# First products by x block of 128 tokens, w2 in two loads, and an input verdict summed over a DMA row, in a Strassen ReGLU MLP kernel

## The chip, the cores and the metric

The kernel runs on one core of a Trainium2 chip. The metric is the device time of one execution in microseconds (us). The kernel before took 309.98 us, the median of its first three runs (309.86 to 310.02). Positions are microseconds from the start of the profiled span, which is about 1.8 us shorter than the time of the same execution.

## The reference

Shortened:

```python
def setup_inputs():
    batch, seq, dim, hidden = 16, 256, 512, 2048
    return {"x": randn(batch, seq, dim), "w1": randn(dim, hidden * 2), "w2": randn(hidden, dim)}   # all float32

def reference(x, w1, w2):
    h = x @ w1
    gate, value = np.split(h, 2, axis=-1)
    h = np.maximum(gate, 0) * value
    return (h @ w2).astype(np.float32)
```

So there are 4096 tokens, two matrix products, and a gate between them.

## The kernel before

The kernel computes both products in fp16 with Strassen-Winograd: seven half-size products P1 to P7 in place of eight, which needs sums of weights (T1 to T4) and sums of activations (S1 to S4). It goes through four stages of 1024 tokens. The first stage must also turn x on TensorE (transposes) and turn fp32 weights into fp16 operands while TensorE is already multiplying. Its first two blocks of hidden columns are therefore "Plain" blocks (ordinary products, no sums needed), and block 2 is the first Strassen block. The engines are scheduled by hand: the order of the calls is the order of each engine.

One Strassen block. ScalarE copies the first product X to Y, because both go on from it; TensorE's later products wait for that copy:

```python
        def P1(self):
            self.X = psx.tile([P, TH], F32, name="X", tag="X")
            self.mm("P1", self.X, True)
            self.Y = psy.tile([P, TH], F32, name="Y", tag="Y")
            nc.scalar.copy(out=self.Y, in_=self.X)
        # ... P5, P2, P6, P3, P7, P4: two products each, then one operation of ScalarE or VectorE
```

The start: the dummy products (TensorE work whose result nobody needs, done while it waits for its first loads), the loads, and the first Plain products of 256 or 512 columns:

```python
    for i in range(NWARM):                     # NWARM = 7
        nc.tensor.matmul(Y, warm_b[:, :P], warm_b[:, :TH], start=True, stop=True)
    # ...
    fetch_first(0, (0, 1))                     # x blocks of 128 tokens
    ws[0] = load_w1(nc.sync, *wl[0], (0,))     # gate weights of block 0
    fetch_first(0, (2, 3))
    load_w1(nc.sync, *wl[0], (1,))             # value weights of block 0
    fetch(1, nc.sync)
    # ...
    keep_busy(3)
    plain[0].open(W=False)
    plain[0].part("gate", *first_half, half)   # 256 columns: waits for two turned x blocks
    turn_first(xo, 0, 2, halves(*XS), (dve, act))
    turn_first(xo, 0, 3, halves(new_w(), new_w()), (dve, act))
    keep_busy(2)
    plain[0].part("gate", *first_half, other)
    # ... later: halves of the x sums, in this order of all four
    SUMS_X = {"S1": ("A21", "A22", ADD), "S2": ("S1", "A11", SUB), "S4": ("A12", "S2", SUB), "S3": ("A11", "A21", SUB)}
```

The streaming weights: GpSimd makes T1 to T4 of each chunk of w1, ScalarE casts the other three operands (`copy_some`), and w2 comes as four converting loads issued by GpSimd; two of GpSimd's subtractions make w2's T1 and T2:

```python
    if 5 <= todo < 9:
        n2 = ("B11", "T3", "B22", "B21")[todo - 5]
        nc.gpsimd.dma_start(out=vop[n2], in_=w2_v[(0, 0, 1, 1)[todo - 5], (0, 1, 1, 0)[todo - 5]])
    if (s, n, jb) == (0, "P7", 13):
        nc.gpsimd.tensor_tensor(vop["T1"], vop["T3"], vop["B11"], op=SUB)
        nc.gpsimd.tensor_tensor(vop["T2"], vop["B22"], vop["T1"], op=SUB)
```

The input verdict. The fp16 way is only right for inputs of ordinary size. Sums of squares are gathered in `st`; in the last stage they are judged, counted over the 128 partitions, and the program branches to a slow general way if any is out of range. With these inputs it never is. The count over partitions is a product of one column on TensorE:

```python
    def count(fit):
        n = P * st.shape[1]
        ps = psx.tile([P, TH], F32, name="X", tag="X")
        nc.tensor.matmul(ps[:1, :1], fit[:, :1], fit[:, 1:], start=True, stop=True)
        nc.vector.tensor_scalar(out=flag, in0=ps[:1, :1], scalar1=n - 0.5, scalar2=None, op0=LT)
    # ... in the last stage, at numbered steps of its second product:
            job(18, lambda: verdict.append(judge()))
            job(46, lambda: count(verdict[0]))
            job(78, lambda: verdict.append(nc.values_load(flag[0:1, 0:1], ...)))
```

Of the kernel before, what the change touches and what calls it, by code (L numbers as in the profile page):

```python
# [16 lines left out]
P = 128  # L17
# [79 lines left out]
def fast_way(ctx, tc, x2, w1, w2, out2, flag):  # L97
# [30 lines left out]
    w2_v = w2.rearrange("(u hc p) (v n) -> u v p hc n", u=2, v=2, p=P)  # L128
# [3 lines left out]
    vop = {n: wpool.tile([P, NJ // 2, DO // 2], F16, name=f"v_{n}") for n in ("B11", "B21", "B22", "T1", "T2", "T3", "T4")}  # L132
# [48 lines left out]
    def look_whole(t, at, of, half=False):  # L181

        sq = tmp.tile([P, 1024], F16, name="sq", tag="sq", bufs=1)
        nc.scalar.activation(sq[:, :of], t, SQUARE, scale=(P / of / (2 if half else 1)) ** 0.5,
                             accum_out=st[:, at:at + 1])
# [52 lines left out]
    class Block:  # L238
        def __init__(self, xo, g, jb):
            self.xo, self.g, self.jb = xo, g, jb  # L240
# [27 lines left out]
        def P3(self):  # L268
# [3 lines left out]
            nc.vector.scalar_tensor_tensor(out=self.c12, in0=self.W, scalar=GS, in1=self.u2, op0=MULT, op1=ADD)  # L272
            nc.vector.scalar_tensor_tensor(out=self.g[:, self.jb, :TH], in0=self.X, scalar=0.0,  # L273
                                           in1=self.c12, op0=MAX, op1=MULT)

        def P7(self):
            self.mm("P7", self.Y, False)
            nc.vector.scalar_tensor_tensor(out=self.c22, in0=self.Y, scalar=GS, in1=self.p5, op0=MULT, op1=ADD)  # L278
            second_halves()
# [170 lines left out]
    def plain_w(i):  # L450
        jb, n, _ = wl[i]
        t = ws.pop(i)
        js = slice(jb * P, (jb + n) * P)
        for n, k, v in (("B11", 0, 0), ("B21", 1, 0), ("T3", 0, 1)):
            nc.gpsimd.tensor_copy(out=wop[n][:, :, js], in_=t[:, k, :, v])
        return lambda: nc.scalar.copy(out=wop["B22"][:, :, js], in_=t[:, 1, :, 1])
# [49 lines left out]
    ws[0] = load_w1(nc.sync, *wl[0], (0,))  # L506
    fetch_first(0, (2, 3))
    load_w1(nc.sync, *wl[0], (1,))
    fetch(1, nc.sync)
# [10 lines left out]
    def halves(*ts):  # L520
        return [t[:, :2 * P] for t in ts]
# [4 lines left out]
    rest = plain_w(0)  # L526
    turn_first(xo, 0, 0, halves(*YS), (dve, act))
    XS = [new_x(), new_x()]
    turn_first(xo, 0, 1, halves(*XS), (dve, act))
    arm(YS[0])  # L530
    arm(YS[1])
    keep_busy(3)
    plain[0].open(W=False)
    plain[0].part("gate", *first_half, half)
    turn_first(xo, 0, 2, halves(*XS), (dve, act))
    turn_first(xo, 0, 3, halves(new_w(), new_w()), (dve, act))
    keep_busy(2)
    plain[0].part("gate", *first_half, other)
    plain[0].W = new_w()
    rest()  # L540
    rest = plain_w(1)
    plain[0].part("value", *first_half)
# [3 lines left out]
    rest()  # L546
    fetch(4, nc.sync)
    plain[0].gate(0)
    plain[1].part("value", *first_half)
    spare = plain[0].X, plain[1].W  # L550
    cast_first(0, pool)
    cast_first(1, dve)
    cast_first(2, pool)
    turn_first(xo, 1, 0, (turns(YS[0])[0], turns(YS[1])[0]), (dve, act))
    turn_first(xo, 1, 1, (turns(plain[0].X)[0], turns(plain[0].W)[0]), (dve, act))
    plain[1].value()
    held = plain[1].held(0)
    cast_first(3, dve)
    xo["S3"] = halfs.tile([P, 8, P], F16, name="xh", tag="xh").rearrange("p (a b) c -> p a (b c)", a=2)
    sums = [sums_of({n: t[:, :, slice(*c)] for n, t in xo.items()}) for c in (half, other)]  # L560
    next(sums[0])
    plain[0].open()
    plain[0].part("gate", *second_half, half)
    turn_first(xo, 1, 2, turns(spare[0]), (act, act))
    turn_first(xo, 1, 3, turns(spare[1]), (dve, dve))
    plain[0].part("value", *second_half, half)
    plain[1].open(*reversed(YS))
    plain[1].part("gate", *second_half, half)
    plain[1].part("value", *second_half, half)
    next(sums[1])  # L570
    next(sums[0])
    next(sums[1])
# [191 lines left out]
```

## Time and profile before

| | before |
|---|---|
| time, first three runs | 309.98 us |
| span of the profiled run | 308.2 us |
| TensorE busy | 301.5 us (98%), 1863 matmuls |
| last matmul ends | 303.50 us |
| end, counted from there ("the tail") | 4.65 us |

TensorE is the bound: the chain that ended last is 97% TensorE. The change removes no real product, so it can only win the holes between products. Those waits are few. TensorE's waits in the kernel before (what waited, for whom, total us, times, longest):

```profile
PE Y L145 <- DVE warm L141: 1.3, 1, 1.3
PE X L314 <- DVE x_S L488: 0.3, 1, 0.3
PE X L245 <- ACT Y L252: 0.3, 1, 0.3
```

The first is the program's own start. The third is the largest hole in the steady part. In the timeline of TensorE it looks like this (start, duration, engine, line, operation, idle before and its releaser); the starts go up by 0.43 us for two products of 512 columns, and then once by 0.85:

```profile
28.70 0.59 PE L245 MATMUL W<-x_S,w_T 128*128 128x512 f16 x2
29.13 0.60 PE L245 MATMUL Y<-xh,w_T 128*128 128x512 f16 x2
29.98 0.59 PE L245 MATMUL X<-x_A,w_B 128*128 128x512 f16 x2 [0.26 <-ACT Y L252]
```

Another hole, at 64.37, comes from a first sum of g (the gated hidden layer, the input of the second product) on VectorE that takes 1.38 us, while its fellows take 0.69. VectorE's timeline, kernel before:

```profile
62.93 1.38 DVE L165 TENSOR_TENSOR w_stage<-g 128x1024 f16<-128x1024 f16 x1
64.41 0.69 DVE L165 TENSOR_TENSOR w_stage<-w_stage,g 128x1024 f16<-128x1024 f16 x1
```

It runs beside this subtraction on GpSimd (GpSimd's timeline, same kernel), which ends at 63.76:

```profile
59.70 4.06 POOL L671 TENSOR_TENSOR v_T<-v_B,v_T 128x2048 f16<-128x2048 f16 x1
```

The Trainium skill, page "SBUF — State Buffer", section "Who interferes with whom", says that a VectorE instruction with two inputs in SBUF contends with a GpSimd instruction that reads SBUF, and that the one that issues second is blocked. This trace agrees that the second one is slowed: 1.38 us against 0.69.

### The profile page before, as it was taken

Reading aid. Unit: us, or ns where it says so; the run is one execution under the profiler, and the core shown is the slowest. Engines: PE = TensorE matmul, PEld = TensorE weight load, DVE = VectorE, ACT = ScalarE, POOL = GpSimd, SP = SyncE. Lnnn points to the kernel's source line nnn. Section 1 sums busy time; section 2 is a strip of 40 time slices with the busy share of each in tenths; the row PEclk is TensorE's granted clock in tenths of the full one; section 3 lists DMA queues with packets and bytes.
Section 4 is the critical chain, followed back from the end, with each engine's and each line's share of the span. In section 5 each row is a group of like instructions: output and inputs, shape, how many; then the busy total and the mean of one; then the engine's idle time right before and its main releaser. Section 6 shows DMA issues by size and latency. Waiting matters only on the chain.

```text
span 308.2 us, 5215 instructions
## 1 busy us (share of the span) xinstructions
PE 301.5 (98%) x1863; PEld 182.4 (59%) x1863; DVE 235.8 (77%) x383; ACT 176.7 (57%) x350; POOL 154.7 (50%) x192
## 2 busy tenths in 40 slices
PE   8999999999999999999999999999999999999993
PEld 5644444588844444478864444458884444448883
DVE  1589888889778888887537888889536888888841
ACT  2598885455865555537855555546865555553230
POOL 1399999920058999400028958910007988700000
PEclk9999999999999999999999999999999999999999
DMA  7977797983784143001354910000335110001132
GB/s 233 353 233 215 211 238 90 191 164 82 213 253 95 66 73 64 2 0 54 137 181 93 188 67 4 0 0 22 117 106 168 35 36 1 0 3 34 53 120 72
DMA packets 37916, 32.87 MB, mean 107 GB/s; under 512 B 14464, under 2 KB 33408, under 8 KB 37760
## 3 DMA queue, kind: packets, MB, share of 16 engines
q1 hardware_dynamic: 33536, 26.22, 28.0%
q0 software_dynamic: 4352, 6.29, 12.1%
q8 instruction: 15, 0.25, 0.4%
q14 instruction: 13, 0.11, 0.1%
HBM read 27.26 MB, written 12.58 MB: 129 GB/s over the span
## 4 chain that ended last, share of the span: by engine, by line
PE 97%; DVE 1%; ACT 0%; issue 0%; DVEq 0%
PE Y L245 26%; PE X L245 17%; PE W L245 17%; PE Y L351 14%; PE W L351 9%; PE X L351 8%; PE Y L145 1%; PE X L314 1%; PE W L314 1%; PE Y L314 1%; DVE w_stage L165 0%; PE X L485 0%; PE Y L485 0%; DVE x_A L488 0%; DVE g L288 0%; PE Y L502 0%
## 5 line engine op out<-in xcount | busy, mean ns | idle before, releaser
L245 PEld LDWEIGHTS <-w_T 128*128 128x128 f16 x496 | 48.4, 98 | 56.9 <-POOL w_T L227 0.3
L175 POOL TENSOR_TENSOR fold<-xh 128x1024 f32<-128x1024 f16 x16 | 30.3, 1894 | 92.2 <-DMA xh<-x 91.4
L245 PE MATMUL X<-x_A,w_B 128*128 128x512 f16 x248 | 73.8, 379 | 0.3 <-ACT Y L252 0.3
L245 PE MATMUL Y<-x_S,w_T 128*128 128x512 f16 x220 | 65.5, 379 | 0.0
L245 PEld LDWEIGHTS <-w_B 128*128 128x128 f16 x372 | 36.3, 98 | 42.6 <-issue 1.1
L272 DVE SCALAR_TENSOR_TENSOR cc<-W,pu 128x512 f32<-128x512 f32 x62 | 42.8, 691 | 20.4 <-ACT pu L266 19.6
L252 ACT COPY Y<-X 128x512 f32<-128x512 f32 x62 | 35.4, 570 | 38.0 <-PE X L245 37.7
L266 ACT ACTIVATE pu<-Y 128x512 f32<-128x512 f32 x62 | 37.0, 597 | 33.8 <-PE Y L245 32.8
L178 POOL TENSOR_TENSOR fold<-fold 128x512 f32<-128x512 f32 (+2 forms) x96 | 51.7, 539 | 7.5
L351 PEld LDWEIGHTS <-w_stage 128*128 128x128 f16 x512 | 49.8, 98 | 6.5 <-DVE w_stage L165 0.6
L278 DVE SCALAR_TENSOR_TENSOR cc<-Y,pu 128x512 f32<-128x512 f32 x62 | 42.8, 691 | 6.6
L273 DVE SCALAR_TENSOR_TENSOR g<-X,cc 128x512 f16<-128x512 f32 x62 | 42.9, 691 | 2.3
L288 DVE SCALAR_TENSOR_TENSOR g<-Y,cc 128x512 f16<-128x512 f32 x62 | 42.2, 681 | 1.8 <-PE Y L245 1.8
L351 PEld LDWEIGHTS <-g 128*128 128x128 f16 x384 | 37.5, 98 | 8.3
L259 ACT ACTIVATE pu<-W 128x512 f32<-128x512 f32 x62 | 37.2, 599 | 0.2 <-ACT Y L252 0.2
L245 PE MATMUL W<-x_S,w_B 128*128 128x512 f16 x124 | 36.9, 379 | 0.0
L245 PE MATMUL W<-x_S,w_T 128*128 128x512 f16 x124 | 36.9, 379 | 0.0
L245 PE MATMUL Y<-x_A,w_T 128*128 128x512 f16 x124 | 36.9, 379 | 0.0
L351 PE MATMUL Y<-v_T,w_stage 128*128 128x256 f16 x256 | 33.2, 273 | 0.0
L351 PE MATMUL X<-v_B,g 128*128 128x256 f16 x256 | 31.9, 273 | 0.0
L165 DVE TENSOR_TENSOR w_stage<-g 128x1024 f16<-128x1024 f16 x32 | 22.1, 705 | 0.2
L383 DVE SCALAR_TENSOR_TENSOR o<-W,pu 128x256 f32<-128x256 f32 x16 | 6.8, 422 | 18.4 <-PE W L351 18.4
(103 smaller groups left out, 291.3 us busy)
## 6 DMA issues: line engine op xcount, KB each, us to landing
w_stage<-in_w_dram SPq DMA_DIRECT2D x14, 512.0 KB, 6.3
out_dram<-o SPq DMA_DIRECT2D x26, 256.0 KB, 2.0
x<-in_x_dram POOLq DMA_DIRECT2D x4, 1024.0 KB, 9.3
xh<-x SPq DMA_DIRECT2D x16, 256.0 KB, 3.4
v_B<-in_w_dram POOLq DMA_DIRECT2D x3, 512.0 KB, 6.1
out_dram<-o SPq DMA_DIRECT2D x12, 128.0 KB, 1.7
w_stage<-in_w_dram SPq DMA_DIRECT2D x4, 256.0 KB, 5.2
x_S<-in_x_dram SPq DMA_DIRECT2D x4, 256.0 KB, 5.9
```

The source lines that it names most:

```text
L165: eng.tensor_tensor(o[n], o[i0], o[i1], op=op)
L175: nc.gpsimd.tensor_tensor(fold, t, t, op=MULT)
L178: nc.gpsimd.tensor_tensor(fold[:, :, :m], fold[:, :, :m], fold[:, :, m:2 * m], op=ADD)
L245: nc.tensor.matmul(ps, wop[wn][:, b, self.jb * P:(self.jb + 1) * P], self.xo[xn][:, b, :], start=fresh and b == 0, stop=b == 1, skip_group ...
L252: nc.scalar.copy(out=self.Y, in_=self.X)
L259: nc.scalar.activation(self.p5, self.W, COPY, scale=GS)
L266: nc.scalar.activation(self.u2, self.Y, COPY, scale=GS)
L272: nc.vector.scalar_tensor_tensor(out=self.c12, in0=self.W, scalar=GS, in1=self.u2, op0=MULT, op1=ADD)
L273: nc.vector.scalar_tensor_tensor(out=self.g[:, self.jb, :TH], in0=self.X, scalar=0.0, in1=self.c12, op0=MAX, op1=MULT)
L278: nc.vector.scalar_tensor_tensor(out=self.c22, in0=self.Y, scalar=GS, in1=self.p5, op0=MULT, op1=ADD)
L288: nc.vector.scalar_tensor_tensor(out=self.g[:, self.jb, TH:], in0=self.Y, scalar=0.0, in1=self.c22, op0=MAX, op1=MULT)
L351: nc.tensor.matmul(ps, self.op[an][:, i], vop[wn][:, i], start=name in ("P1", "P5") and i == 0, stop=i == NJ // 2 - 1, skip_group_check=True)
```

## The change

The intent, in five parts:

1. Start: the first products go by x block of 128 tokens as each is turned, the value weights' load moves ahead of x blocks 2 and 3, the last outputs of the Plain blocks are put off into block 2, and the third x sum S3 gets a tile of its own and is made earlier, in halves.
2. One weight copy on ScalarE, the one that waits for a load before 29.98, is skipped at that place.
3. w2 in two loads of whole rows (1 MB each of fp16) in place of four of 512 KB, and half of w2's T2 moves from GpSimd to VectorE.
4. Some late sums move by a few steps.
5. The verdict's count leaves TensorE: 128 partial counts go to DRAM by one DMA, come back as a row on one partition by another, and VectorE adds the row.

The diff, cut to its core:

```diff
-    vop = {n: wpool.tile([P, NJ // 2, DO // 2], F16, name=f"v_{n}") for n in ("B11", "B21", "B22", "T1", "T2", "T3", "T4")}
+    vop = {n: wpool.tile([P, NJ // 2, DO // 2], F16, name=f"v_{n}") for n in ("T1", "T2", "T4")}
+    w2_rows = [wpool.tile([P, NJ // 2, DO], F16, name=f"w2_{u}") for u in range(2)]
+    vop.update({n: w2_rows[u][:, :, v * DO // 2:(v + 1) * DO // 2]
+                for n, u, v in (("B11", 0, 0), ("T3", 0, 1), ("B21", 1, 0), ("B22", 1, 1))})
 ...
     fetch_first(0, (0, 1))
-    ws[0] = load_w1(nc.sync, *wl[0], (0,))
+    first_w = [load_w1(nc.sync, *wl[0])]
     fetch_first(0, (2, 3))
 ...
-    keep_busy(3)
-    plain[0].open(W=False)
-    plain[0].part("gate", *first_half, half)
-    turn_first(xo, 0, 2, halves(*XS), (dve, act))
+    plain[0].open()
+    plain[0].part("gate", *first_half, cols(0, 2))
+    plain_w(0, 1, (pool, dve))
+    keep_busy(4)
+    plain[0].part("value", *first_half, cols(0, 2))
+    turn_first(xo, 0, 2, halves(*XS, c=2 * P), (dve, act))
 ...
+    for b in (2, 3):
+        for which in ("gate", "value"):
+            plain[0].part(which, *first_half, cols(b), False)      # 128 columns each
 ...
+    for n in ("S3", "S2"):
+        sum_of(sums[0], n)
 ...
+    for n in ("S1", "S2", "S3"):
+        sum_of(sums[1], n)
 ...
-    def count(fit):
+    def gather(fit):
+        fits = dram.tile([P, 1], F32, name="fits", bufs=1)
+        nc.sync.dma_start(out=fits, in_=fit)
+        return fits
+
+    def as_row(fits):
+        row = wpool.tile([1, P], F32, name="row")
+        nc.sync.dma_start(out=row, in_=fits.rearrange("p o -> o p"))
+        return row
+
+    def count(row):
         n = P * st.shape[1]
-        ps = psx.tile([P, TH], F32, name="X", tag="X")
-        nc.tensor.matmul(ps[:1, :1], fit[:, :1], fit[:, 1:], start=True, stop=True)
+        total = wpool.tile([1, 1], F32, name="total")
+        nc.vector.tensor_reduce(out=total, in_=row, axis=mybir.AxisListType.X, op=ADD)
 ...
-                    if 5 <= todo < 9:
-                        n2 = ("B11", "T3", "B22", "B21")[todo - 5]
-                        nc.gpsimd.dma_start(out=vop[n2], in_=w2_v[(0, 0, 1, 1)[todo - 5], (0, 1, 1, 0)[todo - 5]])
+                    if todo in (5, 6):
+                        nc.gpsimd.dma_start(out=w2_rows[todo - 5], in_=w2_v[todo - 5])
 ...
-                    nc.gpsimd.tensor_tensor(vop["T2"], vop["B22"], vop["T1"], op=SUB)
+                    sum_w2(nc.gpsimd, "T2", "B22", "T1", 0)        # the first half; VectorE makes the second
 ...
-                    copy_some(1)
+                    copy_some(0 if (s, n, jb) == (0, "P6", 5) and copies[0][0] == 5 else 1)
 ...
-            job(46, lambda: count(verdict[0]))
+            job(30, lambda: verdict.append(gather(verdict[0])))
+            job(45, lambda: verdict.append(as_row(verdict[1])))
+            job(64, lambda: count(verdict[2]))
```

## The prediction

> **What bounds the kernel now.** TensorE. The page gives PE 301.5 of 308.2 us busy, and the chain of waits is 97% PE. From 1.28 us to 303.50 us the products follow one another: the timeline shows 216 ns from start to start for 512 columns and 109 ns for 256. The change removes no product, so it can win only the holes between starts. Summing every excess over those spacings in the timeline of PE after the first transpose at 4.24 us, I find about 2.3 us:
> - start phase (to 24 us): 0.24 at 8.7, 0.43 at 12.6 (waits for x copies), 0.06 at 13.4, then 0.11, 0.18 and 0.11 at 17.6, 18.7 and 21.8 (ScalarE and VectorE are late with the first Strassen block), plus 0.26 in the dummy products;
> - 0.42 at 29.98: ScalarE runs a weight copy that waits for a load landing at 28.80, so the copy of X that the next product needs comes late;
> - 0.24 at 64.37: the first g sum on VectorE takes 1.38 us instead of 0.69, because it runs beside GpSimd's 4.06 us w2 difference (59.70 to 63.76) and ends 0.55 us after it. The Trainium skill, "SBUF — State Buffer", section "Who interferes with whom", says a VectorE operation with two SBUF inputs and a GpSimd one that reads SBUF exclude each other; this trace agrees;
> - 0.18 at 75.9 and 76.8 (late g sum and output sum);
> - 0.19 at 288.8: the counting product itself, with its one-column load.
>
> **What the change does.**
> 1. Start: first products by 128 tokens. 48 products of 128 columns replace 12 products' worth of wider ones. The f16 transposes of 128 columns follow one another every 55 ns with a weight load each, so this costs almost nothing (the skill's TensorE page, "Back-to-back issue gap", says about 81 ns with loads; this trace says 55). Dummy products stay five. The value weights' load moves ahead of x blocks 2 and 3; loads land every 0.7 to 1.2 us, so value weights land near 6.2 us, not 8.22, and block 3 near 8.2. I expect most of the holes at 8.7 and 12.6 to go, new ones of 0.05 to 0.15 to come. But the gain is capped: the first Strassen block needs T1 and T2, which GpSimd makes from the load landing at 15.71 (T1 15.86 to 16.87, T2 16.95 to 17.95, each 1.0 us instead of 0.67 beside VectorE sums); its product starts at 18.05. TensorE arriving earlier waits there. Net of the start, with the deferred output halves: about 0.45 us by 24 us.
> 2. The weight copy skipped once: the hole at 29.98 goes, 0.42.
> 3. w2 as two loads: two GpSimd issues (about 1 us each) fewer, off the path. Half of the second w2 difference goes to VectorE: GpSimd ends before the first g sum, so 0.24 goes; VectorE's extra 0.7 us fits before its next deadline.
> 4. Reordered late sums: 0.15 of the 0.18.
> 5. Verdict by a DMA row: 0.19 off TensorE; two small DMAs (stores here land in 2 us) off the path.
>
> **Predicted time.** 309.98 - 0.45 - 0.42 - 0.24 - 0.15 - 0.19 = **308.5 us**, 8 in 10 between 307.7 and 309.5. Faster by over 2%: 0.01; within 2%: 0.98; slower by over 2%: 0.01.
>
> **What would show it.** Timeline of PE: 55 ns between 128-column products; the first Strassen P6 between 17.5 and 18.0 us; no hole near 29.5; the first g sum near 0.7 us; no 1x1 product near 288. POOL: the w2 difference is halved.
>
> **What would make it wrong.** VectorE's longer list at 11 to 17 us (casts, turned copies, half sums) holding up the products of x blocks; new exclusion between its sums and GpSimd's T1; the w2 loads of double size delaying w1 loads; 128-column products slower than 55 ns.

## More of the kernel before

The page of the kernel before: its first line of busy time by engine, the chain of waits followed back from the end, and two of its DMA issues (what, engine, count, KB each, median us from issue to landing):

```profile
PE 301.5 (98%) x1863; PEld 182.4 (59%) x1863; DVE 235.8 (77%) x383; ACT 176.7 (57%) x350; POOL 154.7 (50%) x192
...
PE 97%; DVE 1%; ACT 0%; issue 0%; DVEq 0%
...
v_B<-in_w_dram POOLq DMA_DIRECT2D x3, 512.0 KB, 6.1
out_dram<-o SPq DMA_DIRECT2D x12, 128.0 KB, 1.7
```

## The result

| | before | after |
|---|---|---|
| median | 310.11 us (6 runs, 309.86 to 310.71) | 313.99 us (6 runs, 312.23 to 317.58) |
| span of the profiled run | 308.2 us | 312.5 us |
| TensorE busy | 301.5 us, 1863 matmuls | 300.4 us, 1890 matmuls |
| last matmul ends | 303.50 us | 306.26 us |
| from there to the end | 4.65 us | 6.25 us |

The ratio is 1.0106, with a 95% interval from 1.0075 to 1.0137. Here and below a ratio is the mean time of one kernel's runs over that of the other's runs of the same rounds, so it is not quite the ratio of the medians that I quote. Executions over 1.5% slower than the fastest of the same kernel are left out of the means. The run of 317.58 us was a slow one and is not in the ratio. The change costs about 3.4 us by the medians of the fast runs (313.54 against 310.11), where the prediction had it win 1.5. That lies outside the predicted range. The fast runs of the change lie between 312.23 and 314.46, and the profiled one, at 314.44, is among the slower of them, so its trace shows more loss (4.36 us) than the ratio does (3.3).

The page after, the same lines as before, and what the chain of waits now holds:

```profile
PE 300.4 (96%) x1890; PEld 182.5 (58%) x1890; DVE 236.3 (76%) x388; ACT 176.4 (56%) x348; POOL 151.1 (48%) x189
...
PE 87%; DMA 8%; DVE 2%; SPq 1%; issue 0%; POOL 0%; ACT 0%; POOLq 0%
PE Y L249 26%; PE W L249 17%; PE X L249 17%; PE Y L361 11%; PE X L361 8%; PE W L361 7%; DMA fits<-fit 2%; DMA w_stage<-in_w_dram 2%; DMA x_S<-in_x_dram 2%; DMA row<-fits 1%; DVE w_stage L168 1%; SPq L487 0%; POOL w_T L231 0%; SPq L216 0%; DVE cc L286 0%
...
w<-in_w_dram POOLq DMA_DIRECT2D x2, 1024.0 KB, 12.1
out_dram<-o SPq DMA_DIRECT2D x12, 128.0 KB, 3.4
```

TensorE is busy for 1.1 us less than before, and yet later. The chain went from 97% TensorE to 87%: DMAs have come into it, and two of them (`fits<-fit`, `row<-fits`) are the verdict's "two small DMAs off the path". TensorE's waits, after, are the shortest way to see where:

```profile
PE Y L361 <- DVE flag L659: 2.0, 1, 2.0
PE X L249 <- ACT Y L256: 1.4, 1, 1.4
PE Y L148 <- DVE warm L144: 1.3, 1, 1.3
PE W L324 <- POOL w_T L465: 1.0, 1, 1.0
```

Two waits of 2.0 and 1.4 us are new, and so is one of 1.0 in the start. To see what each is worth I counted the Strassen blocks of the whole program from 0 (14 in the first stage, 16 in each other) and noted how much later than before ScalarE copies each block's first product, in the trace after; the same for the last group of output products ("the last pair"):

| place | after minus before, us | change since the row above |
|---|---|---|
| block 3 | +0.04 | the start: +0.04 |
| block 4 | −0.41 | skipped copy: −0.45 |
| block 10 | +1.17 | **+1.58** |
| block 14 (the first of the second stage) and all to the last pair | +0.69 | the g sums and late sums: −0.48 |
| last pair of the last stage | +2.70 | **+2.01** |
| last matmul's end | +2.76 | +0.06 |
| end of the span | +4.36 | **+1.60** |

So there are three losses, 1.58, 2.01 and 1.60 us, and three things to explain.

**The loss at block 10.** ScalarE's and TensorE's timelines after, around it. First ScalarE:

```profile
48.09 0.62 ACT L235 CAST w_B<-w_stage 128x512 f16<-128x512 f32 x1 [1.72 <-DMA w_stage<-in_w_dram]
48.62 0.58 ACT L256 COPY Y<-X 128x512 f32<-128x512 f32 x1
```

and TensorE, one product that waited for the copy at 48.62:

```profile
49.25 0.59 PE L249 MATMUL X<-x_A,w_B 128*128 128x512 f16 x2 [1.35 <-ACT Y L256]
```

ScalarE works in order. A weight cast stood ahead of the copy that TensorE needed, and waited 1.72 us for a load of w1 that landed at 48.07. In the kernel before, the same load landed at 42.52. This is the same pattern as the hole at 29.98 that the change removed, at another place. The hole at 29.98 is gone: after, products start at 29.17, 29.60 and 30.03, every 0.43 us.

**The loss at the last pair.** VectorE's timeline after:

```profile
292.88 0.69 DVE L168 TENSOR_TENSOR w_stage<-g 128x1024 f16<-128x1024 f16 x1
297.62 0.28 DVE L658 TENSOR_REDUCE total<-row 1x1 f32<-1x128 f32 x1 [4.05 <-DMA row<-fits]
297.93 0.14 DVE L659 TENSOR_SCALAR flag<-total 1x1 int32<-1x1 f32 x1
298.00 0.67 DVE L168 TENSOR_TENSOR w_stage<-g 128x1024 f16<-128x1024 f16 x1
```

VectorE stood 4.05 us before the sum of the row, and everything behind it in its order, above all the sum at 298.00 that a product needs, came late. TensorE's timeline after shows the hole that follows:

```profile
298.62 0.60 PE L361 MATMUL Y<-w,w_stage 128*128 128x256 f16 x4 [2.05 <-DVE flag L659]
```

The releaser named is the flag, but the product starts as the sum of 298.00 ends; VectorE's order carries the delay from one to the other. The row is late because of the first of the two DMAs. The lines of tile `fits`, after (its two DMAs with their issue times, who waited for it, and its landing):

```profile
L647 SPq DMA_DIRECT2D fits<-fit x1: 327/327/327, 286.1 to 286.1; - x1
L652 SPq DMA_DIRECT2D row<-fits x1: 301/301/301, 293.9 to 293.9; - x1
...
  DVE total L658: 4.1, 1
...
DMA to landing us min/median/max: 7.8/7.8/7.8
```

512 bytes, written as 128 pieces of 4 bytes, took 7.8 us to land. The prediction had 2 us for it. The second DMA cannot be issued before. The packets themselves are not slow in the trace: 144 of 4 bytes (the 128 and 16 more) begin 0.82 to 1.01 us after the issue and take 7 to 9 ns each, and the landing comes 6.8 us after the last of them has begun. What fills that time the trace does not show.

**The tail.** The end of the chain of waits, before (start, us, what):

```profile
302.63 0.89 PE Y L351 x8
303.52 0.02 issue
303.54 0.38 ACT o L394
```

and after:

```profile
305.39 0.89 PE Y L361 x8
306.27 0.02 issue
306.30 0.38 ACT o L404
```

Both kernels end alike: a last group of products, a last copy, and the last store. But before, the span ends 4.23 us after that copy (308.15 less 303.92), and after, 5.83 us after it (312.51 less 306.68). In the trace the last store is issued 0.45 us after the last matmul in both, and lands 2.94 us (before) or 4.16 us (after) after it. What else the DMA engines move at that time is TensorE's instructions, in pieces of 16 KB:

| from the last matmul's end, us | before | after |
|---|---|---|
| 16 KB fetch for TensorE | +0.11 | −1.92 and +1.42 |
| last packets of the last store | +2.34 | +3.65 |
| end | +4.65 | +6.25 |

### The profile page after: what moved, and what is told of

The parts are those of the page before. It is cut to its first block, busy times and chain, and to the rows that moved or that the text cites. A ratio compares the mean times of both kernels' runs of the same rounds, so it can differ in the third digit from the quotient of the medians.

```text
span 312.5 us, 5259 instructions
## 1 busy us (share of the span) xinstructions
PE 300.4 (96%) x1890; PEld 182.5 (58%) x1890; DVE 236.3 (76%) x388; ACT 176.4 (56%) x348; POOL 151.1 (48%) x189
## 3 DMA queue, kind: packets, MB, share of 16 engines
q0 software_dynamic: 2272, 6.29, 11.1%
## 4 chain that ended last, share of the span: by engine, by line
PE 87%; DMA 8%; DVE 2%; SPq 1%; issue 0%; POOL 0%; ACT 0%; POOLq 0%
PE Y L249 26%; PE W L249 17%; PE X L249 17%; PE Y L361 11%; PE X L361 8%; PE W L361 7%; DMA fits<-fit 2%; DMA w_stage<-in_w_dram 2%; DMA x_S<-in_x_dram 2%; DMA row<-fits 1%; DVE w_stage L168 1%; SPq L487 0%; POOL w_T L231 0%; SPq L216 0%; DVE cc L286 0%
## 5 line engine op out<-in xcount | busy, mean ns | idle before, releaser
L249 PEld LDWEIGHTS <-w_B 128*128 128x128 f16 x372 | 36.4, 98 | 43.4 <-issue 1.6
L361 PEld LDWEIGHTS <-g 128*128 128x128 f16 x384 | 37.5, 98 | 8.3
L249 PE MATMUL W<-x_S,w_T 128*128 128x512 f16 x124 | 36.9, 379 | 0.1
L249 PE MATMUL W<-x_S,w_B 128*128 128x512 f16 x124 | 36.9, 379 | 0.0
L249 PE MATMUL Y<-x_A,w_T 128*128 128x512 f16 x124 | 36.9, 379 | 0.0
L361 PE MATMUL X<-w,g 128*128 128x256 f16 x256 | 31.9, 273 | 0.0
L168 DVE TENSOR_TENSOR w_stage<-g 128x1024 f16<-128x1024 f16 x32 | 21.4, 683 | 0.2
L231 POOL TENSOR_TENSOR w_T<-w_stage 128x512 f16<-128x512 f32 (+1 forms) x16 | 18.6, 1170 | 2.6 <-DMA w_stage<-in_w_dram 2.5
```

The costliest lines, as they stand in the source:

```text
L168: eng.tensor_tensor(o[n], o[i0], o[i1], op=op)
L249: nc.tensor.matmul(ps, wop[wn][:, b, self.jb * P:(self.jb + 1) * P], self.xo[xn][:, b, :], start=fresh and b == 0, stop=b == 1, skip_group ...
L361: nc.tensor.matmul(ps, self.op[an][:, i], vop[wn][:, i], start=name in ("P1", "P5") and i == 0, stop=i == NJ // 2 - 1, skip_group_check=True)
```

## The theories

- **A (row):** the gather of 4-byte pieces lands late, and VectorE's order turns that into TensorE's hole. Rival: the last stage is slow for another reason (for one, the new instruction order), and the row only shows it.
- **B (w2):** the first 1 MB load of w2 delays the last half of w1 that shares the DMA engines with it. Rival: the moved instruction fetches or the new start delay it.
- **C (tail):** the 27 more matmuls, each with a weight load, move the place where a 16 KB instruction fetch falls, and a fetch beside the last store holds the store up. Rival: the verdict's DMAs or the later branch make the tail.
- **D (start):** the new start is worth something that a bound behind it, the landing of the w1 load that T1 reads, hides. Rival: it is worth nothing.

The Trainium skill, page "Runtime: NRT & Kernel Launch", section "Instruction fetch mechanics", says that an engine's instruction memory is refilled in blocks of 16 KiB, 256 instructions, by a DMA queue of its own, and that a taken branch breaks the prefetch. The trace agrees with the size: the instruction queue's pieces for TensorE are 16384 bytes, and, past the first three, they mostly come every 240 to 270 of its matmuls and weight loads. In what follows, "ordinary fetch" is one of that sequence and "jump fetch" the one at the program's closing branch.

## The experiments

In the tables, "this" and "before" are medians of the same call. "Last pair" and "block N" are the shifts against the trace of the kernel before, as in the table above.

### e1: the change, with the verdict counted by the product again

```diff
-            job(30, lambda: verdict.append(gather(verdict[0])))
-            job(45, lambda: verdict.append(as_row(verdict[1])))
-            job(64, lambda: count(verdict[2]))
+            job(46, lambda: count(verdict[0]))      # judge() and count() as before
```

> The whole change, but the verdict summed by the 1x1 product as before. My theory: the 2.2 us hole in TensorE near 298.6 is VectorE waiting in its own queue for the row to land (row at 297.6, first waited for from 293.6), so here the hole goes and 0.19 us of the product comes back: 2.0 us less by the last matmul than the change, and the last pairs shifted no more than the ones before. The hole of 1.5 us near 49 stays. Rival: the 16 KB instruction fetch that took 4.1 us at 288 (others take 1.0 to 1.5) holds one DMA ring, delays stores and row alike, and comes with the program's length, not with the row: then a hole or late stores remain near 290 to 298 here too. Theory: median 310.5 to 312.0; rival: above 312.

Measured: 312.03 against 310.65, ratio 1.0042 (1.0022 to 1.0063). The hole in the last stage is gone: the last pair stands at +0.81, as do all blocks from 14 on. The hole at 49 stays. TensorE's waits in this run:

```profile
PE X L249 <- ACT Y L256: 1.5, 1, 1.5
PE Y L148 <- DVE warm L144: 1.3, 1, 1.3
```

The tail is 5.89 us. So the row makes the last stage's hole, and neither the hole at 49 nor most of the tail. The median is 0.03 us over the range that I had given for the theory; the trace decides for it.

### e2: the change, with w2 in four loads again

```diff
-                    if todo in (5, 6):
-                        nc.gpsimd.dma_start(out=w2_rows[todo - 5], in_=w2_v[todo - 5])
+                    if 5 <= todo < 9:
+                        n2 = ("B11", "T3", "B22", "B21")[todo - 5]
+                        nc.gpsimd.dma_start(out=vop[n2], in_=w2_v[(0, 0, 1, 1)[todo - 5], (0, 1, 1, 0)[todo - 5]])
```

> The whole change, but w2 in the four half-width loads of before, issued as before. Theory: ScalarE's weight copy at 48.09 waited for the second half of the last w1 load, which landed at 48.07 instead of 42.5 because the first w2 load (1 MB, 98 ns packets) shared the rings with it; with 512 KB loads it lands near 42.5 again, no hole near 49, blocks from 10 on sit 0.4 us earlier than before's instead of 1.1 later. Rival: the hole comes from the start order or the skipped copy (the copy list is one place further behind), and then it stays with four loads. Theory: 1.5 us less than the change, median 311.5 to 313.0.

Measured: 311.55 against 310.65, ratio 1.0039 (1.0015 to 1.0064). TensorE's waits:

```profile
PE Y L145 <- DVE warm L141: 1.3, 1, 1.3
PE Y L358 <- DVE flag L656: 1.2, 1, 1.2
PE W L321 <- POOL w_T L462: 0.3, 1, 0.3
```

The wait at 49 is gone, the row's remains. Block 14 stands at −1.07: without the w2 loss the change's gains are there, more than a microsecond by the middle of the program, and the row then takes them back (last pair +0.11). The gather landed 7.54 us after its issue.

### e3: both undone

Edit: those of e1 and e2 together.

> The change with four w2 loads and with the verdict by the product. Theory: both new holes go (1.5 and 2.0 us, and what the tail lost), the holes that the change closed stay closed (0.42 at 30, 0.24 at 64, 0.2 at 76): 0.8 to 1.0 us faster than before, median 309.0 to 309.6. Rival (the new start costs, or a third thing does): 310 or more.

Measured: 310.27 against 310.65, ratio 1.0007 (0.9982 to 1.0032). I had expected 309.0 to 309.6, so this missed. The profile shows two reasons. In this run the w1 load that T1 reads landed at 16.74 (15.71 in the trace before), and block 3 stood at +0.76. The second comes with the part undone: a new hole of 0.88 us opened at 85.46. With four loads, GpSimd issues the converting load of the next stage's x at about 55 us rather than at 53, x lands at 67.1, its transposing loads end at 83.25, and VectorE's x sums run late ahead of an output sum. Parts of this kernel are coupled by the order of the DMA queues, so a part undone alone does not give a clean difference.

### e4: the kernel before, with the row alone

Edit: part 5 of the change, applied to the kernel before.

> The kernel before with the verdict by a DMA row and nothing else of the change. Theory: a hole of 1 to 3 us in TensorE in the last stage, ended by the VectorE sum of the row, varying with the landing of two small DMAs in series: median 311.5 to 313.5, and more scatter than before's 0.2 us. Rival (the fetch of instructions, or the start, makes the loss): within 0.3 us of before.

Measured: 312.28 against 310.65, ratio 1.0059 (1.0042 to 1.0076). The gather landed 7.7 us after issue; TensorE's hole at 297.92 is 1.39 us; blocks ahead of it stand at +0.81 and the last pair at +2.00, the difference of 1.19 being the hole less the count product that is gone. TensorE's waits name VectorE's sum directly here:

```profile
PE Y L145 <- DVE warm L141: 1.3, 1, 1.3
PE Y L351 <- DVE w_stage L165: 1.2, 1, 1.2
```

So theory A does not need the rest of the change, and its rival falls. This kernel, one part more than before, is slower by about 1.6 us by the medians, with the 0.8 us of the start in its trace belonging to the landing of a load, not to the row.

### e5: e2, with the row counted late

```diff
-            job(64, lambda: count(verdict[2]))
-            job(78, lambda: verdict.append(nc.values_load(
+            job(88, lambda: count(verdict[2]))
+            job(92, lambda: verdict.append(nc.values_load(
 ...
-            job(90, lambda: tc.mark_branch_hint_location("general", "LikelyTaken", [ENG.PE, ENG.DVE, ENG.SP]))
+            job(98, lambda: tc.mark_branch_hint_location("general", "LikelyTaken", [ENG.PE, ENG.DVE, ENG.SP]))
```

> As e2_w2_four_loads, but VectorE takes up the row 24 steps (5.2 us) later, and the flag is read later. Theory: the row lands 6 to 11 us after the judgement's last sum and nothing in TensorE needs it; what cost 1.4 us was only VectorE's place in line. Here the hole ended by the row's sum goes (under 0.2 us), the last pair is shifted as the three before, and the time falls by 1.0 to 1.4 us against e2, unless the late flag read costs at the end. Rival: the row's two DMAs delay the stores themselves, then the last pair is late here too, or the end after the last matmul grows.

Measured: 310.75 against 310.23, ratio 1.0000 (0.9976 to 1.0025). The gather still took 7.5 us, but VectorE no longer stood before the row, and the hole of 1.40 us was gone: the last pair stands at −1.03 where e2 had +0.11. A hole of 0.25 us at 298.20, just over the 0.2 that I had allowed, is left; the trace names no releaser for it. The last matmul ended 0.95 us earlier than in e2. The tail was 6.46 us, so the run gained little. The wait, not the DMA, is what costs in the last stage.

### e6: product, and the two loads of w2 one step later

```diff
-                    if todo in (5, 6):
-                        nc.gpsimd.dma_start(out=w2_rows[todo - 5], in_=w2_v[todo - 5])
+                    if todo in (6, 7):
+                        nc.gpsimd.dma_start(out=w2_rows[todo - 6], in_=w2_v[todo - 6])
```

> Verdict by the product; w2 still in two loads of whole rows, each issued one w1 chunk later, so the last w1 load is issued some 5 us before the first w2 load. Theory (sharing of the rings): the last w1 load lands by 43, ScalarE's copy does not wait, the hole near 49 is under 0.2 us. Rival (the size of the packets or the load's own slowness, whenever it is issued): w1 late all the same. Danger: w2's second half lands near 58 to 60 and the second product waits. Theory: median 0.3 to 1.0 us under before.

Measured: 309.97 against 310.23, ratio 0.9981 (0.9950 to 1.0011). The last w1 load lands at 42.83, before w2 starts, and in TensorE's waits only the program's start is left (the view counts only idle time of the engine, so the hole of 0.30 us that e7 closes is not in it):

```profile
PE Y L148 <- DVE warm L144: 1.3, 1, 1.3
```

Blocks from 14 on stand at −1.11 and the last matmul ends at 302.40, 1.1 us before the kernel before. But the time is hardly better, because the tail is 5.88 us, 1.23 more than before. Two loads of 1 MB are harmless when they come after w1.

### e7: e6, with S3 made whole after the Plain outputs

```diff
-    for n in ("S3", "S2"):
-        sum_of(sums[0], n)
+    sum_of(sums[0], "S2")
 ...
-    for n in ("S1", "S2", "S3"):
+    for n in ("S1", "S2"):
         sum_of(sums[1], n)
 ...
     plain[0].gate(1)
+    sum_of(xo, "S3")
```

> e6 with the third x sum taken out of VectorE's list at 14 to 16 us and made once, whole, after the output half at 17.5 us. Theory: in the change GpSimd's first T1 takes 1.25 us instead of 0.7 because VectorE's sums of two SBUF operands run then, and TensorE waits 0.3 us for it at 17.5; with the list 0.7 us shorter T1 takes 0.7 to 0.9 us and that hole is under 0.1; blocks from 1 on sit 0.2 to 0.3 us earlier relative to the landing of the load that T1 reads. Rival: the start hangs on that landing alone (15.7 to 16.7 in the runs so far) and nothing moves.

Measured: 309.81 against 310.23, ratio 0.9983 (0.9966 to 0.9999). The change's early S3 sums on VectorE had run beside GpSimd's T1, which the first Strassen block needs. GpSimd's timeline in the change:

```profile
16.17 1.25 POOL L231 TENSOR_TENSOR w_T<-w_stage 128x256 f16<-128x256 f32 x1 [2.49 <-DMA w_stage<-in_w_dram]
```

and in e7:

```profile
15.88 0.73 POOL L231 TENSOR_TENSOR w_T<-w_stage 128x256 f16<-128x256 f32 x1 [2.45 <-DMA w_stage<-in_w_dram]
```

T1 went from 1.28 us in e6 (1.25 in the change) to 0.73, and TensorE's hole of 0.30 us at 17.2 went. A hole of 0.12 us is left at 18.33. Block 3 moved from −0.25 to −0.39, less than the 0.2 to 0.3 us expected. It is the same contention as at 64.37 in the kernel before, this time at GpSimd's cost.

### e8: e3, with an unused gather of 4-byte pieces

```diff
+            job(30, lambda: gather(verdict[0]))     # 128 pieces of 4 bytes to DRAM; nobody reads them
```

> e3_both_undone with one DMA more: 128 values of 4 bytes, one from each partition, to a DRAM row at the same step as the verdict's first DMA, and nobody waits for it. In the three runs with the row the 16 KB instruction fetch just after it took 4.1, 3.8 and 3.2 us, in the runs without it 0.9 to 1.2. Theory: the writes of 4 bytes to DRAM hold a ring; so here the fetch takes over 3 us and the stores issued then land over 4 us later, but TensorE has no hole in the last stage. Rival: the fetch is slow by chance or by the row's read, then it takes 0.9 to 1.5 us here.

Measured: 311.07 against 310.23, ratio 1.0018 (1.0001 to 1.0035). There is no hole in the last stage. The gather was issued at 282.6, earlier than in the change (286.1), because it waits for nothing. The 16 KB instruction fetch at 286.77, which takes 0.9 to 1.3 us in runs without the gather, took 2.68 us beside it. That is under the 3 us that I had given for it, and far over the 1.5 of the rival. The issue of a store after it took 1.74 us, and that store landed 3.10 us after it was issued (over 4 expected). So the gather slows other traffic, some 3 us after its last packet had begun (283.7) and even where nothing waits for it. In the change, e2, e4 and e5, where a gather that feeds a row is issued shortly before it, that fetch took 3.1 to 4.1 us.

### e13: e8, with 512 bytes per partition

```diff
-        fits = dram.tile([P, 1], F32, name="fits", bufs=1)
-        nc.sync.dma_start(out=fits, in_=st[:, :1])
+        fits = dram.tile([P, 128], F32, name="fits", bufs=1)
+        nc.sync.dma_start(out=fits, in_=st[:, :128])
```

> e8_gather_unused with 512 bytes from each partition to DRAM instead of 4, unused as well. The gathers of 4 bytes landed 7.8, 7.5, 7.7 and 7.5 us after issue, and the stores issued 2.4 us after them 5.3 to 5.6 us after issue (1.8 without a gather). Theory: writes of 4 bytes to one DRAM row are the trouble; here the landing takes 1.6 to 2.5 us, the store after it 1.6 to 2.2, the instruction fetch 0.9 to 1.6. Rival (one more DMA at that place, of whatever kind): over 4 us for the store or the fetch over 2.5.

Measured: 311.14 in one run; only its profile is used. 128 times as many bytes landed in about a fifth of the 7.5 to 7.8 us. The tile's lines:

```profile
L646 SPq DMA_DIRECT2D fits<-st x1: 422/422/422, 282.6 to 282.6; - x1
...
DMA to landing us min/median/max: 1.6/1.6/1.6
```

The instruction fetch beside it took 0.89 us and the next store landed 1.69 us after its issue. So it is the pieces of 4 bytes that land late, not any store to DRAM at that place. A rival stays untested: the 128 small pieces also lie side by side in one stretch of 512 bytes of DRAM, the large ones do not. The Trainium skill, page "DMA: Bandwidth & Descriptors", section "Specifications", says that a transfer under 512 bytes makes the DMA engine read, modify and write. That would fit; no run here shows the mechanism, only that 4 bytes per partition landed in 7.5 to 7.8 us and 512 bytes in 1.6.

### e9: the kernel before, with its dummies cut in four

```diff
-    for i in range(NWARM):
-        nc.tensor.matmul(Y, warm_b[:, :P], warm_b[:, :TH], start=True, stop=True)
+    for i in range(4 * NWARM):
+        nc.tensor.matmul(Y[:, :P], warm_b[:, :P], warm_b[:, :P], start=True, stop=True)
```

> The kernel before, its 7 dummy products of 512 columns cut into 28 of 128: the same columns, the same time, 42 TensorE instructions more. In before, from the last matmul to the end there are 4.65 us; in the change 6.25, and 5.75 to 6.56 in five variants with its start. There TensorE's list is some 55 instructions longer, a 16 KB instruction fetch comes 1.9 us before the last matmul, and the fetch for the jump at the end comes 1.1 to 2.2 us after it instead of 0.1, beside the packets of the last store: 8 of its packets[...] are up to 1.9 us late. Theory: the number of instructions does it; so here the end after the last matmul grows to 5.7 to 6.6 us and the time by 1.0 to 1.5 us. Rival (stores or queues of the change do it): 4.5 to 5.0 us.

This kernel gives a wrong result: products that later add onto Y find only 128 of its columns opened (relative error 0.10). Measured: 309.96 against 310.52, ratio 0.9987 (0.9962 to 1.0011). The fetches moved to −1.23 and +2.10 us from the last matmul, as expected, but the tail was 4.15 us where I had expected 5.7 to 6.6. The last store slipped past the fetch. So the fetch's place is not the whole of theory C.

### e10: e7, with the branch's hint later

```diff
-            job(90, lambda: tc.mark_branch_hint_location("general", "LikelyTaken", [ENG.PE, ENG.DVE, ENG.SP]))
+            job(106, lambda: tc.mark_branch_hint_location("general", "LikelyTaken", [ENG.PE, ENG.DVE, ENG.SP]))
```

> e7_s3_after_t1 with the branch hint 16 steps (3.5 us) later, 1.3 us before the last matmul and so after the ordinary fetch. Theory: if the fetch for the jump can be asked for only while no other fetch stands before it, it now comes near the last matmul and the store is spared: 4.2 to 5.0 us from the last matmul to the end, 0.9 to 1.4 us less than e7. Rival (the hint does not set when that fetch comes): as e7, 5.7 us, or worse.

Measured: 309.63 against 310.52, ratio 0.9990 (0.9963 to 1.0018). The jump fetch stayed at +1.28 us, and the tail was 5.20. The hint does not set the fetch's place; a miss, and why is open.

### e11: e6, with the start of the kernel before

Edit: the loads, copies and products of the first 24 us put back as they were before the change (about a hundred lines, not shown).

> The change without its start: before's first products, loads and x sums; with the skipped copy, the halved w2 difference, the late sums, two w2 loads one chunk later, the verdict by the product. Theory: the start hangs on the landing of the w1 load that T1 reads, so against that landing the old start loses at most 0.3 us; the holes at 30, 64 and 76 are closed; TensorE's list is as short as before's, so the end takes 4.6 to 5.0 us: median 0.7 to 1.2 us under before, under e7 too. Rival (the new start is worth 0.5 us or more and the end does not depend on the list's length): slower than e7.

Measured: 309.68 against 310.52, ratio 0.9973 (0.9950 to 0.9996). The load that T1 reads landed at 16.66, and block 3 stood at +0.80. The holes at 30, 49, 64 and 76 are absent, so blocks from 14 on stand at −0.07, and the tail was 4.53. Without any of the new start, the kernel is as fast as with it; the start is not where the change's worth lies.

### e12: e7, with the fetch boundary moved

```diff
-    for i in range(NWARM):
-        nc.tensor.matmul(Y, warm_b[:, :P], warm_b[:, :TH], start=True, stop=True)
+    for i in range(4 * (NWARM - 1)):
+        nc.tensor.matmul(Y[:, :P], warm_b[:, :P], warm_b[:, :P], start=True, stop=True)
+    nc.tensor.matmul(Y, warm_b[:, :P], warm_b[:, :TH], start=True, stop=True)
```

> e7_s3_after_t1 with six of its seven dummy products of 512 columns cut into four of 128: the same columns, 36 TensorE instructions more, so the ordinary 16 KB fetch, 1.9 us before the last matmul in e7, comes some 2 us earlier. Theory: the fetch for the jump at the end waits for the ordinary one; with that one out of the way it comes 0.1 to 0.5 us after the last matmul as in before, the last store's packets are not held, and the end takes 4.1 to 5.0 us instead of 5.75: 0.8 to 1.5 us less than e7, median 1.0 to 1.8 us under before. Rival (the long list makes the late fetch late wherever the boundary lies): 5.5 us or more, as fast as e7.

This adds 36 TensorE instructions at the start and changes nothing else; the result is right. Measured: 309.56 against 310.24 with five rounds, ratio 0.9979 (0.9965 to 0.9993). The jump fetch moved to +0.21 us, the last store landed at +2.83, and the tail fell from 5.75 us in e7 to 4.47, with the last matmul ending at 302.30 as against 302.25. The times do not show this gain: the ratio is 0.9979 here and 0.9983 in e7, where I had expected 0.8 to 1.5 us less than e7. The profiled execution (308.65) is the fastest of the six; the others took 309.25 to 310.29.

### e14: the whole change, with the fetch boundary moved

Edit: that of e12, on the change.

> The whole change with nothing but its dummy products cut as in e12: 36 TensorE instructions more, the same columns. Theory: of the change's loss, the end is a part of its own: 6.25 us from the last matmul to the end fall to 4.1 to 5.0 because the ordinary fetch comes earlier and the jump's fetch at 0.0 to 0.5 us; the holes near 49 (1.5) and 298 (1.4 to 2.2) stay; median 1 us under the change, 312.0 to 313.2. Rival (e12's short end was luck): 5.5 us or more.

Measured: 311.63 against 310.23, ratio 1.0038 (1.0016 to 1.0060). The tail was 4.84 us with the row in place, 1.41 less than in the change, so the verdict's DMAs do not make the tail, and that rival falls. The row's hole stayed, at 2.29 us (297.81). But the hole at 49, which I had expected to stay, was absent, which puts the median under the 312.0 to 313.2 expected. The last w1 load landed at 44.59. The 16 KB instruction fetch that had come at 36.56, just as that load and w2's first were being issued, came at 33.14 here. The start was also late in this run: the load that T1 reads landed at 17.18, and a hole of 1.03 us followed at 18.11. The gather was issued after the fetch here, and that fetch took 0.93 us; the gather still landed 7.6 us after its issue.

### e15: e12, with five more dummies cut in two

```diff
-        for _ in range(n):
-            nc.tensor.matmul(Y[:, :TH // 2], warm_b[:, :P], warm_b[:, :TH // 2], start=False, stop=True,
+        for _ in range(2 * n):
+            nc.tensor.matmul(Y[:, :P], warm_b[:, :P], warm_b[:, :P], start=False, stop=True,
```

> e12 with the five later dummies cut in two as well, 10 instructions more. A second look at the same question with the boundary elsewhere. Theory: jump's fetch at 0.0 to 0.5 us after the last matmul, the end 4.1 to 5.0 us. Rival: 5.5 or more. Median 309.0 to 309.7.

Measured: 308.93 against 310.23 (308.83 to 309.15), ratio 0.9956 (0.9938 to 0.9974). This is the fastest of all kernels and beats both. The jump fetch came at +0.11 us and the tail was 4.43. The load that T1 reads was late in the profiled run (16.25), and TensorE still ended at 302.84. That e15 is better than e12 is not shown: the two were timed on different chips, and the best of e12's runs (308.65) is under the best of e15's.

### e16: the kernel before, once more

> The kernel before, unchanged, for a second trace of it. The one trace that I predicted from had the w1 load that T1 reads landing at 15.71 us; three variants with the old start had 16.65, 16.66 and 16.73, the variants with the new start 15.70 to 16.09 in ten of eleven. Theory: 15.71 was a lucky start, and here it lands between 16.3 and 17.0, the first Strassen block 0.6 to 1.0 us later than in the first trace, so the new start is in truth worth some 0.6 us by the landing alone. Rival: 15.7 again, and the late ones belong to the variants.

The kernel before: 310.21 us. The load that T1 reads landed at 16.12, against 15.71 in the first trace; I had expected 16.3 to 17.0. (Of the new start's eleven traces, nine and not ten have it at 15.70 to 16.09; e13 has 16.19.) All blocks stand 0.26 us later than in the first trace, so the first trace was an early one. The holes at 30.0, 64.6 and 289.1 are there again (0.19, 0.49 and 0.19 us), and the tail is 4.66 us. The first two trade with each other: they were 0.42 and 0.24 in the first trace, and their sum is 0.66 there, 0.68 here, 0.65 in e4 and 0.68 in e9.

One of the runs of the kernel before beside e9 took 648.11 us. It counts as slow and is in no ratio.

## What the runs say of the theories

**A, the row: shown.** The hole is in every run with the row counted at step 64 (the change, e2, e4, e14: 2.21, 1.40, 1.39 and 2.29 us) and in none with the product; with the row counted late (e5) 0.25 us are left. The gather landed in 7.5 to 7.8 us (the change, e2, e4, e5, e14), in each 6.5 to 6.8 us after its last packet had begun; e13 puts that down to the 4-byte pieces or to their lying side by side.

**B, the w2 loads: shown in part, with a second cause that I had not thought of.** When the last half of w1 lands, by run:

| w2's loads | 16 KB fetch for TensorE at | last w1 load lands | hole at 49 |
|---|---|---|---|
| four (before, e16) | elsewhere | 42.52, 42.57 | no |
| four (e4, e9) | 44.41, 40.36 | 43.48, 44.21 | no |
| four (e2, e3, e5, e8, e13) | 36.5 to 37.5 | 44.9 to 46.4 | no |
| two, early (e14) | 33.14 | 44.59 | no |
| two, early (change, e1) | 36.56, 36.58 | 48.07, 48.18 | 1.5, 1.6 us |
| two, later (e6, e7, e10) | 36.3 to 36.9 | 42.8 to 43.4 | no |
| two, later (e11, e12, e15) | elsewhere | 43.36, 42.21, 42.96 | no |

ScalarE needs the load at about 46.4 us (48.09 less the 1.72 us that it stood idle). The landings also hold how late each start was, so the time from issue to landing is the better measure. It is 5.6 to 6.0 us where w2 comes in four loads or later and the fetch falls elsewhere (before, e16, e4, e11, e12, e15), and 6.6 in e9. With the fetch but no w2 load beside it, it is 6.2 to 6.8 (e6, e7, e10); with the 1 MB load and no fetch, 7.0 (e14, one trace); with the fetch and a 512 KB load, 8.3 to 9.0 (e2, e3, e5, e8, e13); with the fetch and the 1 MB load, 11.1 and 11.2 (the change, e1). So either cause alone costs 0.3 to 1.4 us, and the load has 3.9 to spare (42.52 against 46.4). Together they delay its landing by 5.6 us, and the hole opens. SyncE's issue of the load took 968 ns in the change and 459 before. In the packets, the load is first starved and then shares (w1's column counts all of SyncE's queue):

| packets begun in the trace, us | before: w2 / w1 | after: w2 / w1 |
|---|---|---|
| 38 to 40 | 2 / 618 | 20 / 493 |
| 40 to 42 | 328 / 389 | 223 / 4 |
| 42 to 44 | 710 / 2 | 271 / 171 |
| 44 to 46 | 630 / 0 | 240 / 242 |

After, from 44 us on the two queues get about one packet each in turn. The skill's page "DMA: Bandwidth & Descriptors", section "Queues, rings and completion order", says that each DMA engine goes round its queues packet by packet; the counts 240 and 242 agree. The two microseconds from 40 to 42, with 223 packets against 4, do not look like turns. A stretch of 0.5 to 1.9 us in which w2's packets run and w1's do not is in all seven runs where a fetch and a w2 load come beside the issue of this load (the change, e1, e2, e3, e5, e8, e13), whatever the size of the w2 load, and in no other. So it goes with the fetch; why is open.

**C, the tail: shown in the traces by moving it, less clearly in the times.**

| runs | fetches from the last matmul, us | tail, us |
|---|---|---|
| before, e16 | one, +0.1 | 4.65, 4.66 |
| e4, e11, e12, e14, e15 | one, +0.1 to +0.3 | 5.01, 4.53, 4.47, 4.84, 4.43 |
| change, e1, e2, e5, e6, e7, e8, e13 | ordinary about −2, jump +1.1 to +2.2 | 5.75 to 6.56 |
| e10 | ordinary about −2, jump +1.28 | 5.20 |
| e3, e9 | same pattern | 4.19, 4.15 |

With the boundary moved, the tail was short in all three tries (e12, e14, e15), and with a fetch between the last store's issue and its landing it was long in nine runs of eleven. In all nine, the last eight packets of the last store begin as the fetch ends, within 0.02 us: in the change the fetch runs from +1.42 to +3.00 us and the eight begin at +2.98. This fits one DMA engine doing both in turn; the kept trace does not name engines. In e3 and e9 no packet waited: all of the store's had begun by +1.90 and +2.00 us, with the fetches starting at +1.78 and +2.10. Why the eight waited in e1 and e5, where the fetch starts later still (+2.14 and +2.21), is open. The times say less than the traces: e14 is 2.1 us below the change by the ratios, but its hole at 49 went as well; e15's ratio (0.9956) is below e7's (0.9983), on another chip and with intervals that overlap; e12's (0.9979) is not clearly below.

**D, the start: the rival is nearly right.** How far block 3 stands from the trace of before, less how much later the load that T1 reads landed, is −0.11 to −0.16 us in four runs with the old start (e4, e9, e11, e16), and −0.24 to −0.28 in seven with the new one (the change, e1, e3, e5, e6, e8, e13). So the new start is worth about 0.15 us against that landing. With S3 out of T1's way it is −0.40 to −0.43 (e7, e10, e12), about another 0.14. Two runs lie off these groups but fit by what T1 took: 1.25 to 1.28 us in the seven, 0.73 in e7, e10, e12 and in e2 (at −0.40), and 0.81 in e15 (at −0.34). In e2, T1 began at 16.05, just before VectorE's sum at 16.08, and the sum paid (1.24 us); in the change VectorE's sums had begun first (15.82 and 16.16), and T1 paid. A third is e14 at −0.80, where the load was so late that T1 no longer ran beside any VectorE sum and took 0.73 us; so the sizes are rough. The landing itself lies anywhere from 15.70 to 17.18 us over the runs, which is more than either.

## Why the prediction was wrong

The predicted sum was −1.47 us; the trace shows +4.36. Term by term, with the prediction's own words:

1. *"about 0.45 us by 24 us"* (the start): wrong in size. It measured +0.04 in the trace, about −0.15 against the landing of the load. The prediction named this cap ("the first Strassen block needs T1 and T2") and also the danger ("new exclusion between its sums and GpSimd's T1"), and charged nothing for either; T1 took 1.25 us instead of 1.01. It also put the value weights' landing "near 6.2 us": they landed at 7.14, and a hole of 1.19 us stands at 7.77, hidden behind the same bound.
2. *"the hole at 29.98 goes, 0.42"*: right, 0.45 (in the other traces of the old order the hole is 0.19 to 0.25, so the exact size is luck; its sum with the next is not).
3. *"so 0.24 goes"* (g sum) and *"0.15 of the 0.18"* (late sums): right. Together they measured 0.48 with the 0.39 predicted. VectorE's timeline after has the first sum at its plain price:

```profile
64.06 0.69 DVE L168 TENSOR_TENSOR w_stage<-g 128x1024 f16<-128x1024 f16 x1
```

4. *"two GpSimd issues (about 1 us each) fewer, off the path"*: the failed step of part 3. The issues are off the path, but the loads' bytes are not: +1.58 us at block 10. The prediction listed "the w2 loads of double size delaying w1 loads" as a risk, without asking which w1 load was in flight beside them or who waits for it. Even so the load's slack would have been enough, had an instruction fetch not fallen on the same moment.
5. *"0.19 off TensorE; two small DMAs (stores here land in 2 us) off the path"*: the main failed step. The stores whose 2 us were read from the profile write 1 KB packets; this one writes 4-byte pieces and landed in 7.8 us. And a DMA is not off the path if an engine that works in order stands before its result: VectorE counted the row at step 64 and TensorE needed the sums behind it, +2.01 us.
6. The tail does not appear in the prediction at all: +1.60 us, which goes with where TensorE's instruction fetches fall after 27 matmuls and their weight loads more.

What was right besides: TensorE as the bound, and the products of 128 columns. Of the 48 of them, 43 are followed by the next product after 55 or 56 ns in the trace after, as the transposes were before.

With the row undone, the w2 loads later, S3 later and the fetch boundary moved, the kernel runs in 309.56 us (e12) or, with more of the dummies cut, 308.93 (e15), near the 308.5 that was predicted for the change as it stood.

## What to carry to other kernels

Before a small DMA is called "off the path", look at the size of its pieces, not only at its bytes, and at what stands behind its reader in that engine's order. When a load is made larger or moved, list the loads that are in flight beside it and how much each has to spare before its reader needs it. In a kernel that is 98% bound by TensorE, a few dozen instructions more can move a 16 KB instruction fetch onto a load or onto the last store (here 27 matmuls and their weight loads did), so look at the fetches in the trace before a microsecond is blamed on the change itself.

## What the Trainium skill lacked or had wrong

- "DMA: Bandwidth & Descriptors" says of transfers under 512 bytes that they are read, modified and written, and gives about 2.0 us as the fixed cost of a DMA on the GpSimd path; it gives no time for a store of 4 bytes per partition. From SyncE one of 128 pieces of 4 bytes landed in 7.5 to 7.8 us, one of 128 pieces of 512 bytes in 1.6 us, and a 16 KB instruction fetch beside the former took 2.7 to 4.1 us instead of 0.9 to 1.3.
- "Runtime: NRT & Kernel Launch" calls the cost of crossing a 16 KiB boundary mostly hidden. Here a fetch beside the last store went with a tail 1.1 to 1.9 us longer than the 4.65 us of before in eight runs of eleven (and 0.55 longer in one), and one beside the issue of a 512 KB load of w1 went with 8.3 to 9.0 us from issue to landing where a 512 KB load of w2 ran beside it (6.2 to 6.8 without), against 5.6 to 6.0. No page gives what a fetch costs the data that moves beside it.
- "TensorE: Matmul & The Clock Gate" gives about 81 ns between matmuls of 128 columns with a weight load each; these traces show 55 to 56 ns, near the 56 that the page has for the isolated case.
- "DMA: Bandwidth & Descriptors" describes turns between queues packet by packet. From 44 to 46 us the trace's counts fit that (240 packets of w2 and 242 of w1); from 40 to 42 they are 223 and 4, which no page explains.
